# A hybrid S5/mLSTM encoder step on one core: the first FFN by Strassen's algorithm and by weight rows, the S5 weights made elsewhere

## The chip, the cores and the metric

The kernel runs on one core of a Trainium2 chip. The metric is the device time of one execution in microseconds (us). Engines: PE multiplies matrices into PSUM, eight banks of 128 x 512 fp32; DVE (VectorE), ACT (ScalarE) and POOL (GpSimd) do element-wise work; SP only issues DMAs here, and POOL and ACT issue some too. Each engine takes its instructions in the order of its own queue.

## The reference

One layer of a streaming encoder over 1072 frames (16 learned meta frames, 1024 prompt frames, 32 frames of a second stream) of width 1024, all in fp32:

```python
x = x + 0.5 * swiglu(rmsnorm(x), gate1, up1, down1)        # swiglu(x) = (silu(x@gate) * (x@up)) @ down, inner width 2816
proj = rmsnorm(x) @ w_in                                   # u, xm, z, 1024 each
y5 = s5_mix(u)      # 64 groups of 16 channels, a diagonal complex recurrence of 64 states each, then GELU and GLU
ym = mlstm_mix(xm, z)   # causal conv, block-diagonal q/k/v, gates, matrix memory of 4 heads in chunks
x = x + concat(rmsnorm(y5), rmsnorm(ym)) @ w_out
x = x + 0.5 * swiglu(rmsnorm(x), gate2, up2, down2)
return rmsnorm(x), and the final states of both streams
```

## The kernel before, in words

Everything is kept transposed: `x` is eight tiles of 128 channels x 1072 tokens. A product of two fp32 matrices is made of three matmuls in a reduced type, since each operand is split in a high part (ACT, rounding) and a low part (DVE, the rest): high x high, high x low, low x high. A weight tile of 128 x 1024 is loaded by SP and split by `wslot` (L136, two buffers each of `wr`, `wh`, `wl`); its products with a block of tokens are one `unit` (L164, 24 matmuls into one bank).

The first FFN is `ffn` (L260). It runs over 11 groups of two of the 22 inner tiles: gate and up units for three token blocks of 358, 358 and 356, then this group's share of the down product, added to `x` on DVE (L314). `Prep` makes the norm beside it: `split` (L191) multiplies by the gain and splits, `sq` sums squares (L1482), `fin` makes a column of sums (L220), a reciprocal root on DVE and a row over all partitions (L230). The last group goes block by block, so that the next norm is made beside it.

Into the first FFN a generator `fill` is woven, two or three steps per inner tile: first `ml_fold` (L680; eight times four small matmuls that fold the q, k, v matrices), then `s5_prep` (L505). That one makes tables of the recurrence on DVE and ACT (`s5_tables`, L418), and then for each of 16 batches of four groups: loads of B and C (`raw`, one buffer, eight DMAs on SP), products on POOL into `bb`, `cc`, `lb`, `wo` (L511), on PE the kernel matrix `kp` and four transposes `wps` (L556, L568), which are evicted and stored as `strip` and `win_d`, and the rotation tables `E`, seven doublings and a rest of six products each on POOL, stored as `rot_d`.

The input projection for the mLSTM (`ml_in`, L705) runs over eight 128-channel tiles: a unit for each block, the convolution on DVE (L721), small products `vp` and `gp`, stores of v by POOL's queue. Then `ml_gates` is a long chain on DVE.

The second FFN has its gate and up by `gate_up` (L336) and the class `Strassen` (L1251): pairs of inner tiles, the contraction cut in two halves, the tokens in two pairs of quarters of 264. Per pair of weight tiles and pair of quarters there are 7 products of 12 matmuls (L1376) instead of 8. `weights` makes sums of quarters of the weights on POOL and DVE (L1346 to L1349) and splits them; `late` and `early` make the operand sets of `x`. The result goes to DRAM as `h_d`. `down` (L374) then keeps all eight output tiles of a token block in the eight banks and goes over the 22 weight rows (L398).

The order on each engine's queue is set by a scheduler that follows the program's order as priority and its own estimate of when each instruction is ready; `issue_after`, `behind` and `later` add an order by hand.

## Time and profile before

| | us |
|---|---|
| median of three runs | 2453.95 (2449.87 to 2455.27) |
| the profiled execution, its own time | 2452.73 |
| its span, first to last instruction | 2451.0 |
| PE, DVE, ACT, POOL busy | 2372.5, 1436.2, 861.4, 972.5 |
| mean granted clock of PE | 0.986 of full speed |

A row of the trace gives times from the start of the span. "Busy" counts the time in which at least one instruction of the engine runs; matmuls overlap, so the mean length of one (0.33 us) is longer than the pitch at which they follow each other.

### The profile page before, as it was taken

The page shows a single profiled execution, that of the slowest core. Times are in us where ns is not written, and L with a number is a line of the kernel's source. Part 1 is how long each engine was busy: PE and PEld are TensorE (multiplying, and loading weights), DVE is VectorE, ACT ScalarE, POOL GpSimd, SP SyncE. Part 2 cuts the span into 40 slices and gives each one's busy share as a digit, 9 for nine tenths or more (in the row PEclk, how much of TensorE's full clock was granted, in tenths as well). Part 3 has the DMA queues.
Part 4 walks back from the last instruction along what each step waited for, and adds up shares of the span by engine and source line. Part 5 has one row for each costly group of instructions (what it writes and reads, how often), then busy time and mean ns, then how long its engine had stood idle before and what let it go on. Part 6 is the DMA issues. An engine that isn't in the chain of part 4 may idle for free.

```text
span 2451.0 us, 40952 instructions
## 1 busy us (share of the span) xinstructions
PE 2372.5 (97%) x15656; PEld 2307.7 (94%) x15656; DVE 1436.2 (59%) x2858; ACT 861.4 (35%) x1576; POOL 972.5 (40%) x1790
## 2 busy tenths in 40 slices
PE   8999999999999999999998989999899999999998
PEld 7999999999999988979897989999899999999998
DVE  6446444444444665635778787487765656545663
ACT  5112111111111433323544414564543434334542
POOL 3003777877877522112215262122544444420010
PEclk9999999999999999999999999999899999999999
DMA  4111222242222333252235563122222222265653
GB/s 155 56 50 57 73 75 78 78 113 75 69 78 72 103 119 60 79 161 71 70 133 177 175 191 120 52 66 89 74 75 84 74 84 75 75 209 188 228 180 110
DMA packets 163469, 254.17 MB, mean 104 GB/s; under 512 B 38289, under 2 KB 108961, under 8 KB 163273
## 3 DMA queue, kind: packets, MB, share of 16 engines
q1 hardware_dynamic: 144392, 219.85, 28.7%
q0 software_dynamic: 10032, 27.32, 3.2%
q10 hardware_dynamic: 8848, 4.38, 0.7%
q8 instruction: 123, 2.02, 0.3%
q14 instruction: 74, 0.60, 0.1%
HBM read 192.96 MB, written 62.72 MB: 104 GB/s over the span
## 4 chain that ended last, share of the span: by engine, by line
PE 68%; POOL 11%; DVE 9%; DMA 5%; issue 4%; ACT 2%; SPq 1%; POOLq 0%; ACTq 0%; DVEq 0%
PE psg L161 35%; PE psg L1376 18%; PE psd L398 7%; POOL E L511 3%; POOL et L511 2%; DMA win_d<-wi 1%; PE psg L410 1%; DVE xl L197 1%; PE cps L916 1%; DMA rb<-rb_d 1%; PE nu L884 1%; POOL wo L511 1%; PE vp L730 1%; POOL lb L511 1%; DVE xl L1287 1%
## 5 line engine op out<-in xcount | busy, mean ns | idle before, releaser
L161 PE MATMUL psg<-xh,wh 128*128 128x358 f32 (+4 forms) x2272 | 428.0, 327 | 8.7 <-ACT xh L196 7.9
L161 PE MATMUL psg<-xl,wh 128*128 128x358 f32 (+4 forms) x2272 | 421.8, 325 | 0.0
L161 PE MATMUL psg<-xh,wl 128*128 128x358 f32 (+4 forms) x2272 | 419.2, 324 | 0.0
L161 PEld LDWEIGHTS psg<-xh,wh 128*128 128x128 f32 x2272 | 371.4, 190 | 18.9 <-ACT xh L196 9.7
L161 PEld LDWEIGHTS psg<-xl,wh 128*128 128x128 f32 x2272 | 371.8, 190 | 4.9 <-issue 4.4
L161 PEld LDWEIGHTS psg<-xh,wl 128*128 128x128 f32 x2272 | 371.1, 189 | 3.7 <-issue 3.3
L153 ACT ACTIVATE wh<-wr 128x1024 fp32r<-128x1024 f32 (+1 forms) x182 | 190.9, 1049 | 401.8 <-PE psg L161 266.7
L154 DVE TENSOR_TENSOR wl<-wr,wh 128x1024 fp32r<-128x1024 f32 (+1 forms) x182 | 229.1, 1259 | 121.3 <-ACT wh L153 84.0
L314 DVE SCALAR_TENSOR_TENSOR x<-psg,x 128x358 f32<-128x358 f32 (+1 forms) x264 | 137.9, 528 | 99.3 <-PE psg L161 98.7
L161 PE MATMUL psg<-hh,wh 128*128 128x358 f32 (+1 forms) x528 | 133.7, 334 | 0.9 <-DVE x L314 0.9
L161 PE MATMUL psg<-hl,wh 128*128 128x358 f32 (+1 forms) x528 | 132.1, 329 | 0.0
L161 PE MATMUL psg<-hh,wl 128*128 128x358 f32 (+1 forms) x528 | 129.9, 327 | 0.0
L349 POOL TENSOR_TENSOR sil<-sil,Ra 128x264 f32<-128x264 f32 x88 | 79.1, 914 | 120.6 <-ACT sil L348 120.5
L398 PE MATMUL psd<-hh,wh 128*128 128x360 f32 x352 | 113.8, 327 | 0.7 <-ACT hh L370 0.7
L398 PE MATMUL psd<-hl,wh 128*128 128x360 f32 x352 | 113.8, 327 | 0.0
L273 DVE TENSOR_TENSOR gt<-psg,Ra 128x358 f32<-128x358 f32 (+1 forms) x66 | 34.9, 529 | 128.2 <-PE psg L161 120.8
L1232 POOL TENSOR_TENSOR x<-x,Rb 128x360 f32<-128x360 f32 (+1 forms) x11 | 10.9, 1018 | 245.4 <-ACT Rb L231 245.4
L282 DVE TENSOR_TENSOR hf<-sil,psg 128x358 f32<-128x358 f32 (+1 forms) x66 | 34.8, 527 | 123.4 <-PE psg L161 123.4
L1482 POOL TENSOR_TENSOR acc<-acc,sq 128x358 f32<-128x358 f32 (+2 forms) x36 | 38.5, 1069 | 170.5 <-ACT sq L1480 169.9
L511 POOL TENSOR_TENSOR et<-E 128x8 f32<-128x8 f32 (+6 forms) x256 | 92.8, 362 | 19.1
L161 PEld LDWEIGHTS psg<-hh,wh 128*128 128x128 f32 x528 | 92.5, 190 | 2.5 <-DVE x L314 2.3
L161 PEld LDWEIGHTS psg<-hl,wh 128*128 128x128 f32 x528 | 94.3, 190 | 0.0
(422 smaller groups left out, 4979.3 us busy)
## 6 DMA issues: line engine op xcount, KB each, us to landing
wr<-w2f SPq DMA_DIRECT2D x44, 512.0 KB
wr<-win SPq DMA_DIRECT2D x24, 512.0 KB
h_d<-sil SPq DMA_DIRECT2D x88, 132.0 KB
wr<-w1g SPq DMA_DIRECT2D x22, 512.0 KB
wr<-w1u SPq DMA_DIRECT2D x22, 512.0 KB
wr<-w1d SPq DMA_DIRECT2D x22, 512.0 KB
x<-w2g SPq DMA_DIRECT2D x22, 512.0 KB
x<-w2u SPq DMA_DIRECT2D x22, 512.0 KB
```

Source lines behind the costliest of these rows:

```text
L153: nc.scalar.activation(vh, r, AF.Copy)
L154: nc.vector.tensor_tensor(vl, r, vh.bitcast(F32), op=ALU.subtract)
L161: self.nc.tensor.matmul(ps[:, :n], lhsT=a[k], rhs=b[k], start=i == 0, stop=i == 3 * nk - 1)
L197: nc.vector.scalar_tensor_tensor(l, s, gain, h.bitcast(F32), op0=ALU.mult, op1=ALU.subtract)
L273: nc.vector.tensor_tensor(gt[:, :n], ps[:, :n], R[:, t0:t0 + n], op=ALU.mult)
L282: nc.vector.tensor_tensor(hf[:, :n], sil[:, :n], ps[:, :n], op=ALU.mult)
L314: nc.vector.scalar_tensor_tensor(xs, ps[:, :n], 0.5, xs, op0=ALU.mult, op1=ALU.add)
L349: nc.gpsimd.tensor_tensor(g, g, r, op=ALU.mult)
L398: nc.tensor.matmul(ps[o][:, :n], lhsT=l[:, o * P:(o + 1) * P], rhs=r, start=f == i == 0 and l is w[0], stop=f == NF - 1 and l is w[1])
L511: PT = lambda o, x, y, op: nc.gpsimd.tensor_tensor(o, x, y, op=op)
L1376: nc.tensor.matmul(ps[c, bank], lhsT=l[:, k * P:(k + 1) * P], rhs=r[k], start=start and i == k == 0, stop=i == 2 and k == 3, skip_group_ch ...
L1482: e.tensor_tensor(d, d, sq, op=ALU.add)
```

## The change

In the first FFN, gate and up go through `Strassen` with quarters of 268 tokens. `x` is loaded in quarters; `ready` adds the squares and multiplies by the gain in place, and `sets` makes all seven operand sets of both halves at the start. The result goes to a DRAM tile; `x`, overwritten by then, is loaded again in `down1`, which goes by weight rows over three blocks of 358, 358 and 356. The products on POOL of `s5_prep` are woven into `down1`, one step per weight row. Their matmuls are a generator of their own, `s5_pairs`, behind the last matmul of `down1`, with the norm's columns and rows between them. The rotation tables (`s5_rot`, eight groups at once, half of the products on DVE) and `ml_fold` go one step per tile into the input projection. `win_d` and `rot_d` are stored by SP's queue. In the second FFN the held products of the first pair come out after its third product of the second half, not after the first. The weights' host layout changes with it.

```diff
+    def row(self, ps, f, w, h, n):
+        for l, rs in zip(w, (h, h[:1])):
+            for o in range(8):
+                for i, r in enumerate(rs):
+                    self.nc.tensor.matmul(ps[o][:, :n], lhsT=l[:, o * P:(o + 1) * P], rhs=r, start=f == i == 0 and l is w[0], stop=f == NF - 1 and l is w[1])
+
+    def down1(self, x, h_d, wf, blks, post, filler):
+        todo = []
+        for j, (t0, n) in enumerate(blks):
+            ps = self.banks()
+            for f in range(NF):
+                h = self.h_load(h_d, self.hp, f, t0, n, blks[0][1], bufs=4)
+                self.row(ps, f, self.wslot(wf[f]), h, n)
+                if f > 1 and todo:
+                    i, o = todo.pop(0)
+                    post.split(i, o)
+                    post.sq(i, o)
+                if j == 0 and f in range(6, 14):
+                    self.nc.sync.dma_start(x[f - 6], self.a["xT"][f - 6])
+                next(filler, None)
+            for o in range(8):
+                xs = x[o][:, t0:t0 + n]
+                self.nc.vector.scalar_tensor_tensor(xs, ps[o][:, :n], 0.5, xs, op0=ALU.mult, op1=ALU.add)
+                todo.append((j, o))
...
+    def s5_pairs(self, pool):
+        nc, N = self.nc, 4
+        for b in range(16):
+            lb, cc = self.lb[:, b], self.cc[:, b]
...
-            wi = pool.tile([P, 512], F32, tag="lb2", name="wi")
+            wi = lb.rearrange("p g s h -> p (g s h)")
             nc.scalar.activation(wi, wps, AF.Copy)
-            nc.gpsimd.dma_start(self.win_d[b].rearrange("(h s) x -> s h x", s=8), wi)
...
+            nc.sync.dma_start(self.win_d[b].rearrange("(h s) x -> s h x", s=8), wi)
+            yield
+
+    def s5_rot(self, pool):
+        nc, N = self.nc, 8
...
+                t, u = (pool.tile([P, N, 64], F32, tag=n_, name=n_)[:, :, :m] for n_ in ("et", "eu"))
...
-                PT(t, ej(1), en(1), ALU.mult)
-                PT(eo(0), ej(0), en(0), ALU.mult)
-                PT(eo(0), eo(0), t, ALU.subtract)
-                t = pool.tile([P, N, 64], F32, tag="et", name="et")[:, :, :m]
+                VT(u, ej(1), en(1), ALU.mult)
+                VT(eo(0), ej(0), en(0), ALU.mult)
+                VT(eo(0), eo(0), u, ALU.subtract)
                 PT(t, ej(0), en(1), ALU.mult)
                 PT(eo(1), ej(1), en(0), ALU.mult)
                 PT(eo(1), eo(1), t, ALU.add)
...
+            st = Strassen(self, W1, xa, xn, Rb, hp)
+            st.open("right", 6)
...
+            def ready(c, q, k):
+                t0 = W1 * (2 * c + q)
+                xs, r = x[k][:, t0:t0 + W1], Ra[:, t0:t0 + W1]
+                if k == 0:
+                    nc.scalar.activation(r, xs, AF.Square)
+                else:
+                    sq = hp.tile([P, W1], F32, tag="sq", name="sq", bufs=2)
+                    nc.scalar.activation(sq, xs, AF.Square)
+                    (nc.gpsimd if k % 2 else nc.vector).tensor_tensor(r, r, sq, op=ALU.add)
+                nc.vector.tensor_scalar(xs, xs, self.v(V_FFN1, k), None, op0=ALU.mult)
...
+            w = st.weights((a["w1g"][0], a["w1g"][1]), lambda: (x_load(0), x_load(1, (0,))))
+            s0 = st.sets(0)
+            for i, n in enumerate((2, 1, 2, 1, 1)):
+                st.w0 = next(w)
...
+                for _ in range(n):
+                    next(s0)
...
+            self.down1(x, h_d[0], a["w1f"], blk, post, self.s5_prep(sp))
+            with self.later():
+                for b, _ in enumerate(self.s5_pairs(sp)):
+                    if b in (2, 5, 8):
+                        post.cols(b // 3)
+                    if b in (4, 7, 10):
+                        post.rows()
...
+                fold, rot = self.ml_fold(mp, mpa, pb), self.s5_rot(pb)
+                next(fold)
+                next(rot)
                 for k in range(8):
+                    next(fold, None)
                     w = self.wslot(a["win"][8 + k])
...
                     self.ml_in(k, w, xn, Rb, blk, pb, xc[k])
+                    next(rot, None)
...
         for i in range(7):
             step(i, 1)
-            if i == 0:
-                rows()
-                for h in held:
-                    out(*h)
+            if i == 2:
+                flush((0, 1) if self.ready is None else (0,))
+            if i == 3 and holds:
+                rows = rest(1)
+            if i == 6 and holds:
+                flush((1,))
```

## Rows read from the trace of the kernel before

**Rows 1.** Page of before, parts 1 and 4: busy us by engine; the chain's shares.
```profile
PE 2372.5 (97%) x15656; PEld 2307.7 (94%) x15656; DVE 1436.2 (59%) x2858; ACT 861.4 (35%) x1576; POOL 972.5 (40%) x1790
...
PE 68%; POOL 11%; DVE 9%; DMA 5%; issue 4%; ACT 2%; SPq 1%; POOLq 0%; ACTq 0%; DVEq 0%
```

**Rows 2.** Windows: stretch, its us, busy (x count) of PE PEld DVE ACT POOL, PEclk, DMA, GB/s.
```profile
6.26:55.00 48.74, 43.26 (x227) 41.33 (x228) 37.59 (x78) 29.41 (x60) 18.58 (x21) 0.89 0.50 162
...
200.00:855.30 655.30, 640.31 (x3919) 635.83 (x3918) 314.80 (x592) 136.15 (x215) 488.85 (x1257) 0.99 0.26 78
...
855.30:1005.50 150.20, 149.66 (x875) 128.00 (x873) 86.81 (x194) 47.66 (x84) 41.82 (x61) 1.00 0.36 93
...
1742.40:2176.40 434.00, 434.00 (x3577) 433.80 (x3576) 263.54 (x406) 178.26 (x365) 197.19 (x175) 1.00 0.27 87
...
2177.10:2351.00 173.90, 173.86 (x1057) 173.86 (x1058) 92.17 (x128) 82.69 (x123) 0.00 (x0) 1.00 0.62 204
```

**Rows 3.** Windows of line L161 on PE in the first FFN: stretch, us, busy (count).
```profile
619.93:631.72 11.79, 11.79 (x74) 1.00 0.15 47
```

**Rows 4.** Timeline of PE where the input projection begins: start, us, what.
```profile
855.30 1.49 PE L161 MATMUL psg<-xh,wh 128*128 128x358 f32 x8
...
867.98 0.81 PE L230 MATMUL R<-ident,ry 128*128 128x128 f32 x6
```

**Rows 5.** Timeline of DVE and POOL before and in the second FFN's first pair.
```profile
1695.71 0.43 DVE L1287 TENSOR_TENSOR B11l<-x,B11h 128x264 fp32r<-128x264 f32 x1
...
1696.22 0.76 POOL L1281 TENSOR_TENSOR x<-x 128x264 f32<-128x264 f32 x1 [9.85 <-DVE B11l L1287]
...
1717.12 8.62 DVE L1287 TENSOR_TENSOR xl<-x,xh 128x264 fp32r<-128x264 f32 x12
...
1717.63 7.14 POOL L1281 TENSOR_TENSOR x<-x 128x264 f32<-128x264 f32 x8 [6.66 <-DVE xl L1287]
...
1726.01 8.83 DVE L1287 TENSOR_TENSOR xl<-x,xh 128x264 fp32r<-128x264 f32 x11
```

**Rows 6.** Groups of DVE in the second FFN's down: busy us, mean ns, idle before.
```profile
L154 DVE TENSOR_TENSOR wl<-wr,wh 128x1024 fp32r<-128x1024 f32 x43 | 52.7, 1225 | 67.9 <-ACT wh L153 41.4 <-PE psd L398 26.5
...
L371 DVE TENSOR_TENSOR hl<-hr,hh 128x360 fp32r<-128x360 f32 x44 | 23.2, 528 | 1.2 <-ACT hh L370 1.1
```

**Rows 7.** Windows of POOL from 200 to 850: all, then tile E alone.
```profile
200.00:850.00 650.00, 485.54 (x1253) 0.99 0.26 79
...
200.00:850.00 650.00, 275.54 (x862) 0.99 0.26 79
```

**Rows 8.** Timeline of the S5 tables: first DVE product, a first POOL product of prep.
```profile
198.85 0.23 DVE L420 TENSOR_TENSOR mag<-lamr,ldt 128x64 f32<-128x64 f32 x1 [0.56 <-ACT ldt L427]
...
208.75 0.29 POOL L511 TENSOR_TENSOR pt<-raw,lami 128x64 f32<-128x64 f32 x1 [0.36 <-DVE lami L479]
```

**Rows 9.** Waits of SP's queue, 200 to 850: us in total, times, longest.
```profile
SPq L526 <- POOL cc L542: 105.1, 14, 10.5
...
SPq L539 <- POOL bb L511: 18.0, 2, 13.6
```

**Rows 10.** Waits of PE, 40 to 856: us in total, times, longest.
```profile
PE kp L556 <- POOL lb L511: 14.0, 9, 3.6
```

**Rows 11.** Timeline of PE, one batch of S5 matmuls and what follows.
```profile
269.75 0.96 PE L556 MATMUL kp<-cc,lb 128*128 128x16 f32 x8
...
270.95 1.54 PE L161 MATMUL psg<-xh,wh 128*128 128x358 f32 x8
```

**Rows 12.** Timeline of PE, one step of the fold and what follows.
```profile
73.94 0.31 PE L697 MATMUL fp<-gq,bd 128*128 128x36 f32 x2
...
74.75 0.58 PE L161 MATMUL psg<-hh,wh 128*128 128x358 f32 x2
```

**Rows 13.** Group of DVE, 855 to 1006: busy us, mean ns, idle before.
```profile
L721 DVE SCALAR_TENSOR_TENSOR cv<-xm,vec,cv 128x1075 f32<-128x1075 f32 x24 | 31.8, 1330 | 1.5 <-ACT cv L719 1.5
```

**Rows 14.** Group of ACT, 855 to 1006.
```profile
L734 ACT ACTIVATE vs<-vp 128x256 f32<-128x256 f32 x8 | 3.1, 385 | 31.0 <-DMA v_d<-vs 24.3 <-PE vp L730 3.9 <-PE psg L161 2.8
```

More of the change, by code (lines that the diff above doesn't have):

```diff
@@ L49, in cuts @@
         t += 2 * q
-    return out
-def down_slots(groups):
-    out, f, off = [], 0, 0
-    for gi, g in enumerate(groups):
-        no = 2 if g == 3 else 4
-        for o in range(0, 8, no):
-            out.append((gi, f, g, o, no, off))
-            off += P * no * g * P
-        f += g
     return out
@@ L372, in h_load, with banks, down @@
         return hh, hl
-    def down(self, x, wf, wd, pool, post):
+    def banks(self):
+        return [(self.psg if o % 2 == 0 else self.psm)("psd") for o in range(8)]
+    def row(self, ps, f, w, h, n):
[21 more added lines that the diff above has]
+                todo.append((j, o))
+        for _ in filler:
+            pass
+        for i, o in todo:
+            post.split(i, o)
+        for i, o in todo:
+            post.sq(i, o)
+    def down(self, x, h_d, wf, wd, pool, post):
         nc, blks = self.nc, post.blks
@@ L1303, in early, with late, sets @@
             self.split(0, "T4", k, b21)
-    def late(self, c):
-        if c == 0:
-            for k in (2, 3):
-                self.split(0, "T4", k, self.rows(0, k)[2])
-            return
-        r = [self.rows(1, k) for k in range(4)]
+    def late(self):
+        for k in (2, 3):
+            self.split(0, "T4", k, self.rows(0, k)[2])
+    def sets(self, c):
+        r = [self.rows(c, k) for k in range(4)]
         for n in self.OPS:
             for k, (b11, b12, b21, b22) in enumerate(r):
+                if self.ready is not None and n in ("B11", "B21", "T1", "T2"):
+                    self.ready(c, n[0] == "T", k + 4 * (n in ("B21", "T2")))
                 if n == "T1":
@@ L1366, in gemm @@
                 K.behind(es, 20)
-                self.late(1)
+                for _ in self.sets(1):
+                    pass
         ps, u, held = {}, {}, []
+        holds = set() if rest is None else {0, 1}
         def mm(c, bank, a, b, start=True):
@@ L1383, in emit @@
         def emit(n, c, q, t):
-            if rest is not None and c == 0:
+            if c in holds:
                 held.append((n, c, q, t))
@@ L1416, in gemm, with flush @@
             step(i, 0)
-        rows = rest()
+        rows = rest(0)
+        def flush(cs):
+            rows()
+            holds.difference_update(cs)
+            for h in held:
+                if h[1] in cs:
+                    out(*h)
         for i in range(7):
             step(i, 1)
-            if i == 0:
-                rows()
-                for h in held:
-                    out(*h)
+            if i == 2:
[4 more added lines that the diff above has]
+                flush((1,))
 class _Spare:
```

298 lines of the change are left out of this document (133 added, 165 removed).

## The prediction

> **What bounds the kernel now.** First the busy times and the chain that ended last: PE is busy 97% of the span and holds 68% of the chain [rows 1]. The reader is to see that a saving must be made in PE's time, or in the gaps of its queue. Second the same by stage [rows 2]: the first FFN (6.26 to 855.3) is PE-bound after its start, the start is not (43.3 of 48.7 us busy at a granted clock of 0.89, and a busy PE there is often a slow one), and the second FFN's gate and up, which already go by Strassen, keep PE busy in all 434.0 us of their steady part. Third PE's pitch, stage over matmuls (an edge of such a window counts one or two matmuls too many): first FFN 11.79/72 = 0.1638 us for three units of 358, 358 and 356 columns; Strassen at 264 columns 434.0/3577 = 0.1213; down by weight rows at 360 columns 173.9/1057 = 0.1645 [rows 2, 3].
>
> **The change, part by part.** All against the profiled execution: span 2451.0, its own time 2452.7, which is 1.2 under the median 2453.95 of three runs. I follow PE's clock to the point where the input projection is alone on PE. Before that is 855.3 plus the three blocks' norm columns and rows still to come, 0.81 for a block's rows [rows 4] and about as much for its columns, together some 4: 859.2.
>
> *Start.* Before, PE's first matmul comes at 6.26, behind one tile of weights and one block of x [rows 2]. After, the first pair of weight tiles needs all seven operand sets of both token halves, made while PE waits. DVE is the longest: per half 28 splits, 16 gain multiplications, 6 additions of squares. One split alone takes 0.43, and POOL's subtraction alone 0.76; side by side, 23 splits take 17.45, 0.76 each [rows 5]. So 28 x 0.76 = 21.2; the additions are like a split, 6 x 0.43 = 2.6; a gain multiplication has no row: under a split's 0.43, over half of it, I take 0.35, 5.6. Two halves 58.8, the weights' own two wide (1.22 [rows 6]) and five half-wide operations (between 0.43 at 264 and 1.22 at 1024 columns: 0.69) 5.9, start at about 6. End of the first pair: 70. Ends: 50 if nothing slows the splits, 86 if POOL's 48 operations of 0.76 all stand in DVE's way.
>
> *Gate and up.* 3168 matmuls at 0.1638 become 22 weight pairs x 2 halves x 7 products x 12 = 3696. At 268 columns the pitch lies between 0.1213 and, by columns, 0.1213 x 268/264 = 0.1231, which I take. The 21 pairs after the first: 3528 x 0.1231 = 434.3, to 504. DVE, ACT and POOL have the same work beside it as in the second FFN, 61%, 41% and 45% busy there [rows 2]; that cover holds.
>
> *Down.* 1584 matmuls stay 1584; by rows at 0.1645 they take 260.6 (before 259.5). With 1 us of hand-over (the two stages of the second FFN lie 0.7 apart [rows 2]): 766.
>
> *S5 weights beside down.* Before, POOL is busy 485.5 between 200 and 850, 275.5 of it with the rotation tables (tile E) [rows 7]. What stays beside down is the rest of 210, less the issue of win_d, which moves to SP: I take 200, in 261 instead of 650 us. In front stand the lambda tables, DVE and ACT work before POOL's first product, 198.85 to 208.75 before [rows 8], 13 with the loads. DVE's operations on two SBUF tiles in that stage: 66 x (1.225 + 0.528) = 116 [rows 6], and 14 for 24 splits and squares like the second. 12 splits and 8 subtractions would take 11.2 one after the other and took 8.62, 0.77 of that [rows 5]; (200 + 130) x 0.77 + 13 = 267 against 261. So POOL has no slack here, where before it was 75% busy. It reaches PE by SP's queue: the loads of `raw`, one buffer, wait for POOL, and behind them stand the loads of weight and h rows. Before, SP stood at these loads 237 us in 30 waits, 7.9 each [rows 9] (the first and the last of four such rows), harmless with one weight load per 12 us. Now a weight row is eaten every 24 x 0.1645 = 3.95 us; two slots are a reserve of 7.9. I take 8 us for the stage, since the mean wait is just the reserve. Ends: 0, and 32 waits as long as the longest at L526, 10.5: 32 x 2.6 = 83. x is loaded a second time (4.4 MB) in eight of these steps; the second FFN does so at the same place, moved 204 GB/s in its stage with PE unbroken [rows 2], so it costs nothing. If that cover goes, one load of 0.5 MB stands before each weight row, 1 to 2 us each.
>
> *Pairs.* The K and win matmuls leave the first FFN with the waits of kp for lb, 14.0 [rows 10]; their PE time stays, 1.2 per group of four (269.75 to 270.95) [rows 11], 16 x 1.2 = 19.2, now behind the last down matmul. With the norm columns and rows between them 4, and 6 for eight evictions of 0.53 (as hl [rows 6]) that free the banks, with splits and squares on DVE: 29. Ends 23 and 45; the input projection's first four units can fill in, further ones wait for a row of Rb. At 8 + 29 behind 766: 803 against 859.2, that is 56 gained.
>
> *Input projection.* The folded q, k, v matmuls come here: 0.81 on PE per k (73.94 to 74.75) [rows 12], 8 x 0.81 = 6.5. The rotation tables come too, half on DVE, 8 batches of 8 doublings x 3 operations on each engine. POOL's 275.5 us are 862 operations of four groups each; after there are eight groups in each and half of the products go to DVE, so a quarter of the operations and half of the elements stay: between 69 and 138, I take the middle, 104. DVE: 0.69 at 512 columns, 0.43 at 264, the rest of the eight widths less each, about 2.3 for the eight; x 3 x 8 = 55. In this stage DVE was 86.8 and POOL 41.8 of 150.2 [rows 2]; that makes 142 and 146. It fits, with nothing over. By 0.77: (31.8 [rows 13], 8 x 1.22 [rows 6] and 55 of DVE on two tiles, 104 of POOL) = 201 x 0.77 = 154, 4 late. Behind a rotation step on POOL queue the v_d stores; for those ACT already waits 24.3 with its copies out of PSUM [rows 14]. On DVE the evictions that free PE's banks and the gates' chain queue behind it. I take 14. Ends 0 and 201 - 150 = 51.
>
> The second FFN's edit (the rows of its norm two products later) is put at nothing: other products stand in the gap.
>
> Sum: -56 + 6.5 + 14 = -35.5, 2452.7 - 35.5 = 2417.
>
> **A rule against it.** DVE's split goes from 0.43 to 0.72 and 0.80 beside POOL [rows 5], so the two hinder each other, but 20 operations still overlapped to 0.77 of their sum. The Trainium skill, "SBUF — State Buffer", section "Who interferes with whom", is harsher: a DVE instruction with two SBUF inputs and a GpSimd instruction that reads SBUF share a port under an exclusive lock, and the second one blocks fully. The trace agrees that they block, not that nothing overlaps. Taken strictly it is the rival "turns" below.
>
> **Rivals.** *Everything fits* (chance 0.20): no stall in down, none by the rotations, banks free in time: 2417 - 8 - 14 - 6 = 2389; with the short start 2369. For it: POOL and DVE work that took no PE time before; against it: both stages come out at 94 to 102% full.
>
> *Turns* (0.05): DVE and POOL never overlap. Down's helpers take 200 + 130 + 13 = 343, 82 late instead of 8; rotations 51 instead of 14; start 86 instead of 70: 2417 + 74 + 37 + 16 = 2544. Against it: 8.62 for 11.2 [rows 5], and 263.5 + 197.2 busy in 434.0 us without a gap on PE [rows 2].
>
> *SP's queue* (0.12), slower than before: in the down stage the raw loads hold up weight rows. Price up to 83 instead of 8: 2417 + 75 = 2492. It decides from (36 + 8)/32 = 1.4 us beyond the reserve per wait. For it: 7.9 mean, 10.5 longest at L526, up to 13.6 at L539 [rows 9]; against: a wait is long where SP had nothing else to do, as it had before.
>
> *It doesn't do what it says* (0.03): narrow matmuls cost as much as wide ones. Then 3528 x 0.041 is lost, 2560; 0.1213 speaks against it [rows 2].
>
> **How the numbers follow.** Forecast 2417 (0.60), its own range 2398 to 2440 from the start's and the pairs' ends. A measurement of this kernel tells about 0.2% (5 us) from no change. Faster: 0.58 of the forecast, 0.20, and 0.02 of SP's queue in a mild form, 0.80. Same: 0.02 + 0.04 + 0.01 = 0.07. Slower: 0.06 + 0.05 + 0.02 = 0.13. The range 2380 to 2462 reaches into everything fits and into half of SP's queue.
>
> **What would show it.** Right: steady gate and up at 0.123 per matmul; the first pair done near 70; down at 0.165 with few gaps; first input projection matmuls near 770 and alone near 800; no kp wait over a few us. Wrong: PE waiting for wl or hh in down with SP at raw; kp waiting for lb; PE below 95% in the input projection with DVE near 100%; a later stage that loses what the first gains.

## The result, and the profile after

The changed kernel takes 2521.3 us (median of 4 runs, 2518.6 to 2524.0) against 2454.6 for the kernel before on the same chip: ratio 1.0274, 95% interval 1.0252 to 1.0296. It is slower by 67 us, where 2417 was forecast and the range ended at 2462. One execution each of experiments 1, 4 and 14 was far longer than its fellows (8924.8, 5033.4 and 2640.1) and is left out of the medians below. The profiled execution has a span of 2521.6, 70.6 longer than [rows 1].

The page of after, busy times and chain, against [rows 1]: PE is busy 5.5 us less, and idle 155 us instead of 79, which is the growth of the span. POOL's largest rows in the chain are `lt` and `wo`, S5 products.

```profile
PE 2367.0 (94%) x16196; PEld 2288.9 (91%) x16196; DVE 1604.6 (64%) x3104; ACT 1015.3 (40%) x1926; POOL 1061.2 (42%) x1336
...
PE 60%; DVE 14%; POOL 11%; issue 6%; DMA 5%; ACT 2%; SPq 1%; POOLq 0%; DVEq 0%; ACTq 0%
PE psg L1414 34%; PE psg L148 10%; PE psd L287 9%; POOL lt L449 2%; PE psg L348 2%; POOL wo L449 2%; POOL lbs L449 1%; DVE xl L1307 1%; PE cps L872 1%; POOL E L534 1%; PE nu L840 1%; POOL bb L449 1%; DMA rb<-rb_d 1%; DVE wl L141 1%; DMA rot_d<-E 1%
```

The forecast followed PE from stage to stage, so the loss is found by the same marks, read from the timelines of PE: first down matmul, last down matmul, last transpose of the gates (`gtp`, end of the input projection), last `nu` (end of the mLSTM). The last two of before are 1008.9 and 1240.1; its down and norm were taken to end at 859.2.

| stretch on PE | forecast | after | difference |
|---|---|---|---|
| start, gate and up, to the first down matmul | 504 | 523.3 | +19 |
| down | 270 | 308.8 (to 832.1) | +39 |
| pairs, entry, input projection, to the last `gtp` | 199 (29 + 149.7 + 6.5 + 14) | 226.8 (to 1058.9) | +28 |
| gates and chunks, to the last `nu` | 231.2, as before | 250.7 (to 1309.6) | +19.5 |
| the rest | as before | 1.1 longer | +1 |

Together 106, which is the forecast's -35.5 turned into +70.6. Windows of after: stretch, its us, busy (count) of PE, PEld, DVE, ACT, POOL, PE's granted clock, DMA share, GB/s.

```profile
0.00:70.00 70.00, 38.40 (x163) 31.40 (x164) 63.83 (x111) 35.88 (x90) 45.74 (x54) 0.92 0.38 124
70.00:95.00 25.00, 20.66 (x111) 19.59 (x112) 17.86 (x37) 11.40 (x28) 10.52 (x11) 0.68 0.07 19
95.00:520.00 425.00, 425.00 (x3445) 425.00 (x3445) 248.67 (x392) 172.07 (x351) 186.43 (x165) 1.00 0.25 78
523.30:832.30 309.00, 275.48 (x1588) 271.03 (x1587) 182.76 (x274) 115.34 (x173) 236.80 (x375) 0.96 0.56 183
580.00:620.00 40.00, 33.63 (x193) 32.75 (x192) 20.04 (x18) 12.62 (x18) 37.91 (x62) 0.96 0.57 185
700.00:740.00 40.00, 35.67 (x196) 35.10 (x197) 26.88 (x31) 18.39 (x31) 38.06 (x62) 0.91 0.56 184
870.00:900.00 30.00, 20.00 (x91) 19.59 (x91) 4.97 (x22) 4.59 (x7) 4.54 (x19) 0.52 0.58 128
```

The reader is to see four things: a start with PE half idle; a steady stretch as forecast (425.0/3445 = 0.1234 us per matmul, 0.1231 forecast); a down stage (523.3 to 832.3) in which PE is idle for 33.5 us and has a mean clock of 0.96, so that its busy time grows too, while POOL is full at 95% in the two windows of 40 us; and 30 us before the input projection with PE idle for a third, at a granted clock of 0.52.

Groups of DVE in the start of after, shapes apart, with mean ns of one:

```profile
L1307 DVE TENSOR_TENSOR xl<-x,xh 128x268 fp32r<-128x268 f32 x32 | 20.6, 667 | 0.0
L952 DVE TENSOR_SCALAR x<-x,vec 128x268 f32<-128x268 f32 x32 | 19.1, 619 | 0.0
L951 DVE TENSOR_TENSOR Ra<-Ra,sq 128x268 f32<-128x268 f32 x12 | 6.8, 563 | 0.0
```

SP's waits from 580 to 835 (us in total, times, longest), and ACT's group for the high parts of the weights in the whole of down:

```profile
SPq L139 <- DVE wl L141: 40.0, 21, 3.5
SPq L466 <- POOL cc L482: 34.1, 14, 5.3
SPq L479 <- POOL bb L449: 24.7, 8, 6.2
SPq L479 <- POOL pt L449: 13.5, 6, 3.7
```
```profile
L140 ACT ACTIVATE wh<-wr 128x1024 fp32r<-128x1024 f32 x67 | 70.9, 1059 | 172.0 <-DMA wr<-w1f 120.3 <-PE psd L287 38.2 <-DVE hl L276 5.3
```

SP stands 72 us at the loads of `raw` for POOL, the weight rows come late behind them (120 us of ACT's idle time ends with a landing weight row), and PE waits for ACT. These are the waits of [rows 9], smaller in sum and each (2.6 in the mean of 28, 6.2 the longest), but now in front of PE. SP's timeline, with the wait of PE that follows:

```profile
588.36 0.38 SPq L139 DMA_DIRECT2D wr<-w1f  x1
...
592.38 2.39 SPq L479 DMA_DIRECT2D raw<-s5c  x4
594.87 0.53 SPq L139 DMA_DIRECT2D wr<-w1f  x1
...
599.77 3.18 SPq L466 DMA_DIRECT2D raw<-s5b  x4
603.00 0.58 SPq L139 DMA_DIRECT2D wr<-w1f  x1
...
608.11 0.43 PE L287 MATMUL psd<-hh,wh 128*128 128x358 f32 x1 [3.90 <-ACT wh L140]
```

From 588.36 to 603.00 one weight row goes out between the two at the ends, where PE eats one in 3.95: two waits for POOL and the issue of eight loads (5.6) stand there. In the whole of down the issue of the 128 loads holds SP for 76 us (0.59 each in the median), as long as its waits for POOL do (77).

The timeline where the input projection begins:

```profile
880.58 1.73 PE L514 MATMUL kp<-ccs,lbs 128*128 128x16 f32 x8
...
882.59 4.74 SPq L523 DMA_DIRECT2D strip<-ks  x8
...
887.44 0.58 SPq L529 DMA_DIRECT2D win_d<-lbs  x1
888.07 1.89 SPq L1017 DMA_DIRECT2D tg_d<-strip  x3
...
892.08 0.11 POOL L539 MEMSET E<- 128x8 f32 x1 [83.44 <-DMA tg_d<-strip]
...
892.14 0.59 DVE L1007 MEMSET GM<- 128x640 f32 x1 [9.58 <-DMA tg_d<-strip]
...
892.66 0.52 DVE L669 TENSOR_TENSOR xm<-psg,Rb 128x358 f32<-128x358 f32 x1
...
893.24 2.16 PE L148 MATMUL psg<-xh,wh 128*128 128x358 f32 x6 [10.01 <-DVE xm L669]
```

`E`, `GM` and `xm` lie where the S5 weights (`lbs`, one tile for all batches) were, so they wait for the last store out of it. DVE stands at GM's memset, and behind it on the queue are the evictions `xm` that free PE's banks. POOL, which was to make rotation tables, has been idle for 83 us.

Behind the input projection some two batches of tables are left, and stand in the queues of DVE, POOL and SP ahead of the gates. Windows of tile E alone in the gates of after (DVE and POOL busy):

```profile
1058.90:1139.70 80.80, 24.21 (x58) 42.27 (x69) 0.96 0.40 133
```

From the last `gtp` to the first `ktp` are 80.8 us instead of 42.0. PE does units of the S5 input there, work that it has to do later in any case, so that only half of it is lost.

### The profile page after: what moved, and what is told of

Read it like the earlier page. It is cut to its first block, busy times and chain, and to the rows that moved or that the text cites. A ratio compares the mean times of both kernels' runs of the same rounds, so it can differ in the third digit from the quotient of the medians.

```text
span 2521.6 us, 43211 instructions
## 1 busy us (share of the span) xinstructions
PE 2367.0 (94%) x16196; PEld 2288.9 (91%) x16196; DVE 1604.6 (64%) x3104; ACT 1015.3 (40%) x1926; POOL 1061.2 (42%) x1336
## 4 chain that ended last, share of the span: by engine, by line
PE 60%; DVE 14%; POOL 11%; issue 6%; DMA 5%; ACT 2%; SPq 1%; POOLq 0%; DVEq 0%; ACTq 0%
PE psg L1414 34%; PE psg L148 10%; PE psd L287 9%; POOL lt L449 2%; PE psg L348 2%; POOL wo L449 2%; POOL lbs L449 1%; DVE xl L1307 1%; PE cps L872 1%; POOL E L534 1%; PE nu L840 1%; POOL bb L449 1%; DMA rb<-rb_d 1%; DVE wl L141 1%; DMA rot_d<-E 1%
## 5 line engine op out<-in xcount | busy, mean ns | idle before, releaser
L287 PE MATMUL psd<-hh,wh 128*128 128x358 f32 (+2 forms) x880 | 291.6, 335 | 30.5 <-ACT wh L140 24.8
L287 PE MATMUL psd<-hl,wh 128*128 128x358 f32 (+2 forms) x880 | 290.2, 333 | 0.0
L148 PE MATMUL psg<-xh,wh 128*128 128x352 f32 (+4 forms) x1216 | 226.7, 324 | 11.8 <-DVE xm L669 10.0
L148 PE MATMUL psg<-xl,wh 128*128 128x352 f32 (+4 forms) x1216 | 228.9, 325 | 0.0
L148 PE MATMUL psg<-xh,wl 128*128 128x352 f32 (+4 forms) x1216 | 221.8, 322 | 0.0
L148 PEld LDWEIGHTS psg<-xh,wh 128*128 128x128 f32 x1216 | 195.2, 192 | 16.7 <-DVE xm L669 10.4
L148 PEld LDWEIGHTS psg<-xl,wh 128*128 128x128 f32 x1216 | 197.6, 193 | 7.6 <-issue 7.3
L287 PEld LDWEIGHTS psd<-hh,wh 128*128 128x128 f32 x880 | 170.2, 194 | 34.6 <-ACT wh L140 28.4
L148 PEld LDWEIGHTS psg<-xh,wl 128*128 128x128 f32 x1216 | 195.7, 191 | 1.1 <-issue 0.8
L287 PEld LDWEIGHTS psd<-hl,wh 128*128 128x128 f32 x880 | 170.4, 194 | 0.0
```

What stands on the lines that cost most here:

```text
L148: self.nc.tensor.matmul(ps[:, :n], lhsT=a[k], rhs=b[k], start=i == 0, stop=i == 3 * nk - 1)
L287: self.nc.tensor.matmul(ps[o][:, :n], lhsT=l[:, o * P:(o + 1) * P], rhs=r, start=f == i == 0 and l is w[0], stop=f == NF - 1 and l is w[1])
```

## The experiments

Ratios are to the kernel before on the same chip, with the 95% interval; after stands at 1.0274.

**1. Is it SP's queue?** Loads of B and C only for the first of 16 batches; the others compute with those values.

```diff
-            raw = new("raw", 2)
+            if b == 0:
+                raw = new("raw", 2)
...
-            craw = new("raw", 2)
+            if b == 0:
+                craw = new("craw", 2)
```

> Left out: the loads of B and C for 15 of the 16 batches; every batch computes with the first one's. POOL's products, DVE's work and the weight rows stay as they are; only the loads that made SP's queue wait for POOL are gone. Changed kernel: down from 523.3 to 832.8, 309.5 us where 1584 matmuls at 0.1645 are 260.6; PE idle in it about 31, granted clock 0.91 to 0.96 in between. If SP's queue is the cause (weight rows behind loads that wait for POOL): idle of PE in the down stage below 5, down 262 to 268, the time 41 to 49 shorter, 2472 to 2481. If DVE and POOL hinder each other at SBUF so that the splits of the weights come late: PE still waits for wh and wl, down stays above 295, the time within 10 of 2521.

1.0109 (1.0081 to 1.0137), 2484.4. Down takes 275.9 instead of 308.8. POOL is as full as before:

```profile
580.00:620.00 40.00, 40.00 (x246) 40.00 (x245) 22.60 (x25) 16.62 (x23) 38.34 (x54) 1.00 0.60 204
...
740.00:780.00 40.00, 40.00 (x247) 40.00 (x246) 22.37 (x22) 16.86 (x22) 38.19 (x55) 1.00 0.63 209
```

So 33 of the 47 us that down takes over the 262 of experiment 16 are SP's queue. The other 14 (262 to 268 was expected here) stay while POOL makes its products; PE waits 6.5 once for `wh` and 5.0 in two waits for `wl`, and what makes them was not tested. "Turns" falls as well: DVE's work in down takes 145.8 with POOL almost idle (experiment 16) and POOL's some 200 by the forecast, which one after the other would not fit in 275.9.

**2. The rotation tables** left out (memsets in place of the six products).

```diff
-                VT(u, ej(1), en(1), ALU.mult)
...
-                PT(eo(1), eo(1), t, ALU.add)
+                nc.gpsimd.memset(eo(0), 0.5)
+                nc.gpsimd.memset(eo(1), 0.5)
```

> Left out: the products of the rotation tables (constants are stored in their place, by the same queue, from the same tile). From the end of down to the last gate transposes the changed kernel took 29 us more than forecast, and the gates behind them cost 17 more. If the rotations' work on DVE and POOL and the waits for it are the cause: 35 to 50 us shorter, 2471 to 2486. If most of it is the wait of DVE at the entry of the stage (PE idle 10 us for xm, then a granted clock of 0.52) the gain is only 10 to 22: 2499 to 2511, and the 10 us wait stands in the trace as before.

1.0168 (1.0150 to 1.0186), 2498.0: between the two expectations, nearer to the second. The last `gtp` comes only 3 us earlier, while the gates are back at 42.1, and DVE's wait at the entry stands as before (PE waits 10.0 for `xm`). The tables cost about 23 us, nearly all in the gates, not in the input projection. Without the products their stores come in a burst, so the 23 is not a clean price.

**3. The gain multiplication** of the start on ACT.

```diff
-                nc.vector.tensor_scalar(xs, xs, self.v(V_FFN1, k), None, op0=ALU.mult)
+                nc.scalar.activation(xs, xs, AF.Copy, scale=self.v(V_FFN1, k))
```

> The 32 multiplications by the norm's gain at the start go from DVE (0.62 each, 19 us of the 82 in which it is busy without a gap) to ACT. If DVE's queue sets the start: the first pair's last matmul 10 to 16 us earlier than 93.5, the time 8 to 16 shorter, 2505 to 2513. If ACT, with the high parts and the squares, becomes as late (43 of 94 us busy, 13 more), or the transfers of x set it: within 4 of 2521.

1.0217 (1.0201 to 1.0232), 2509.6. The first pair ends at 88.6 instead of 93.5, down begins at 518.4 instead of 523.3. The time lies in the first branch, and in part by luck: the start gives 4.9 where 10 to 16 were expected, and 9 come from the gates and chunks (241.9 for 250.7).

**4. The same products spread** over twice as many weight rows.

```diff
-                next(filler, None)
+                if f % 2 == 0 or j == 0 and f < 2:
+                    next(filler, None)
```

> One step of the S5 weights per two weight rows in place of one per row, over the whole down stage (33 steps for 66 rows); nothing left out. If SP's queue is the cause, the loads of B and C now come at POOL's own pace (about 14.5 us a batch against 4 x 3.95 = 15.8), the down stage loses below 10 us, and the time is 38 to 49 shorter, 2472 to 2483. If the pairs' matmuls then wait for POOL's last batches, up to 20 of it are given back: 2483 to 2503, with waits of kp for lb. If the cause is contention at SBUF: within 10 of 2521.

A miss: 1.0245 (1.0224 to 1.0265), 2516.4; SP still stands 69.5 at POOL's `cc`, `pt` and `bb` between 580 and 835 and down takes 303.8. The edit did not change the order on SP: the batches' first loads go out at 532, 564, 584, 599, 613, and at 532, 565, 585, 600, 614 in after. The place in the program is only a priority; that the scheduler's estimate of POOL is too fast is my reading of it, not shown.

**5. Loads tied to their weight row** on SP, one batch ahead, at the pace of 4, in five buffers (`pin` sets the order behind SP's last DMA).

```diff
+        def load(b):
+            with self.pin():
+                for n in ("s5b", "s5c"):
+                    out.append(pool.tile([P, 2, N, H5], F32, tag="raw" + n, name="raw", bufs=5))
...
+            raw, craw = nxt
+            nxt = load(b + 1) if b < 15 else None
```

> Nothing left out. The loads of B and C get five buffers each instead of one, come one batch ahead, one batch per four weight rows, and are tied on SP's queue behind the weight row before them, so that the scheduler can't draw them forward to where it thinks that POOL will be free. If SP's queue is the cause of the long down stage, this gives what leaving the loads out gave: down 262 to 276 instead of 308.9, the time 32 to 45 shorter, 2476 to 2489, and SP's waits for POOL below 10 us in all. If POOL's work as such is the limit (239 busy of 309), its last batches come after the last weight row and the pairs wait for lb: down 262 to 276, but kp waits of 10 to 25 behind it, 2490 to 2505.

Down misses both branches: 1.0186 (1.0164 to 1.0208), 2501.3; down 288.0. Three batches of eight DMAs, some 0.6 us each, stand in a row on SP at the beginning and hold a weight row up, for which PE waits 12.8:

```profile
550.00:580.00 30.00, 21.26 (x114) 21.26 (x115) 21.25 (x70) 8.96 (x13) 16.29 (x31) 0.77 0.59 180
```

**6. As 5, one DMA per batch** (B and C laid out together on the host).

```diff
+                nc.sync.dma_start(t, a["s5bc"][:, b])
```

> As the one with pinned loads, but B and C of a batch come in one DMA instead of eight (the host lays them out so); nothing else. With eight DMAs a batch, SP needed 5 us to issue them, three batches in a row stood before the third weight row (PE idle 12.8 there), and down took 288 against 276 without the loads. If that is SP's issue time: down 268 to 278, the time 30 to 40 shorter than the changed kernel, 2481 to 2491. If it is the transfers themselves that hold up the weights (many small pieces): down still above 284, 2497 to 2504.

1.0138 (1.0119 to 1.0158), 2489.8; down 272.0. With 16 loads on SP instead of 128 (9 us of issue instead of 76), down is 16 us shorter than in 5, and 10 us over the 262 of experiment 16. The new layout makes the pieces of a load larger too (1 KB of a partition in place of 256 bytes), so issue and transfer are not told apart.

**7. Memory.** The S5 weights in 16 tiles, two buffers for `ks`, the tables `E` on the other side, where the rows of h had been.

```diff
-        self.lb = pool.tile([P, 16, N, 8, H5], F32, name="lbs")
+        self.lb = [pool.tile([P, N, 8, H5], F32, name=f"lbs{b}") for b in range(16)]
...
-                fold, rot = self.ml_fold(mp, mpa, pb), self.s5_rot(pb)
+                fold, rot = self.ml_fold(mp, mpa, pb), self.s5_rot(rp)
```

> Nothing left out. The S5 weights lie in 16 tiles instead of one, ks gets two buffers, and the rotation tile E and its two scratch tiles lie where the h rows of the down stage were, instead of on the S5 weights: so the first eviction of xm need not wait for the last store of win_d, and POOL can begin the rotations at about 832 instead of 892, where it now stands idle for 83 us. If the wait at the entry and the lateness of the rotations (two batches in the gates' way, 80.8 from the last gate transpose to the first chunk's ktp against 42.0 before) are the cause: the wait of 10 for xm goes, the gates take 42 to 48, the time 28 to 45 shorter, 2476 to 2493. If the rotations, drawn into the pairs, stand on DVE in the way of ks and xm (each doubling waits for the other engine): less than 15 gained, 2506 or more.

1.0156 (1.0133 to 1.0178), 2494.0. The tables begin in the stage of the pairs and are done in time: the gates are back at 41.7, with the last `gtp` 4 later (1063.3). The wait for `xm` stays at 8.6, now because a batch of rotations stands ahead of it on DVE's queue.

**8. 3, 5 and 7 together**, and the second load of x tied to its rows too.

```diff
-                    self.nc.sync.dma_start(x[f - 6], self.a["xT"][f - 6])
+                    with self.pin():
+                        self.nc.sync.dma_start(x[f - 6], self.a["xT"][f - 6])
```

> Both edits and the gain on ACT together, and the second loads of x tied on SP's queue behind weight rows 6 to 13 instead of all at the start of the stage. If the losses are separate, they add up: 12 + 38 + 35 and 3 to 6 for the loads of x, 2428 to 2442, faster than before. If they share what they hide (an earlier end of down leaves POOL's prep to end behind it, and the rotations with it): 2445 to 2460.

Above both expectations: 1.0090 (1.0065 to 1.0114), 2478.0; `gtp` 1042.5, gates 41.8. PE waits 10.7 for `xm`, again behind rotations on DVE.

**9. As 8, all rotations on POOL.**

```diff
-        VT = lambda o, x, y, op: nc.vector.tensor_tensor(o, x, y, op=op)
+        VT = PT
```

> As the one with everything, but all products of the rotations on POOL, none on DVE: about 170 us of POOL between the end of down and the gates (220 us with v's stores, 42). If DVE's queue in the input projection is what the rotations cost: 3 to 12 faster than with both engines. If POOL then becomes the limit (its products took 0.55 to 0.65 us in the mean beside DVE, which makes 230): rotations end in the gates again, 5 to 20 slower than with both.

1.0156 (1.0127 to 1.0185), 2492.3. `gtp` comes 18 us earlier (1024.6), the gates take 88.7: POOL's tables run to 1100, and the stores that the gates wait for stand behind them. No rotation stands on DVE's queue, and still PE waits 14.8 for `xm`: DVE's small memset of `xm` waits for a DMA, as in after. The last pairs run at full clock here (0.96 for eight `kp`, 1.73 in after).

```profile
844.71 0.96 PE L528 MATMUL kp<-ccs,lbs 128*128 128x16 f32 x8
...
860.39 0.06 DVE L678 MEMSET xm<- 128x3 f32 x1 [13.74 <-DMA tg_d<-strip]
```

**10. As 9, with one DMA per batch as in 6**, the S5 weights laid out last batch first, two buffers for `E`, the weights of the fold in a free tile of x, the gates' stores by ACT.

```diff
-            E = pool.tile([P, 2, N, SCOL], F32, tag="E", name="E", bufs=1)
+            E = pool.tile([P, 2, N, SCOL], F32, tag="E", name="E", bufs=2)
...
-        nc.gpsimd.dma_start(self.rb_d[0:NH], b)
+        nc.scalar.dma_start(self.rb_d[0:NH], b)
```

> Everything that the runs so far pointed to: one DMA a batch, the gain on ACT, x's second loads tied to weight rows, the S5 weights in 16 tiles laid out last batch first (so that the first xm lies on batches stored long before), all rotations on POOL with two buffers of E (with one, POOL waited 6 to 8 us for each store), the gates' rows stored by ACT's queue instead of POOL's. If the losses are what the runs say: down 268 to 276, no wait for xm, the last gate transpose at 995 to 1012, gates of 42 to 50, and 2425 to 2452, faster than before or level. If the rotations on POOL again end in the gates and hold up the first chunk: 2455 to 2475.

Above both expectations: 1.0184 (1.0170 to 1.0198), 2500.5. The wait for `xm` is gone (0.55; PE waits 4.3 for `bd`). The input projection ends at 999.8, 9 us before that of the kernel before, and all of it is given back: PE waits for `bq`, whose work stands behind the tables on POOL.

```profile
836.60 2.75 PE L155 MATMUL psg<-xh,wh 128*128 128x358 f32 x8 [0.55 <-DVE xm L678]
```
```profile
PE ktp L810 <- DMA bq<-bqk: 35.8, 1, 35.8
```

**11 to 15. The share of DVE and POOL.** Whole batches, instead of half of each, go to one engine: three of eight to DVE in the first.

```diff
-        PT = lambda o, x, y, op: nc.gpsimd.tensor_tensor(o, x, y, op=op)
+            e = nc.vector if b in (1, 3, 5) else nc.gpsimd
+            PT = VT = lambda o, x, y, op, e=e: e.tensor_tensor(o, x, y, op=op)
```

> As the best guess before it (there the input projection ended at 999.8, 9 before the kernel before, and then the first mLSTM chunk waited 35.8 for rotations still on POOL until 1100), but rotation batches 1, 3 and 5 wholly on DVE and the other five wholly on POOL, so that neither waits for the other inside a batch; and every second bd tile in a free row of x. Five batches on POOL at about 27 plus v's stores 27 make some 165 us from 812, so they end near 1000, before the gates. If that is the whole trouble: last gate transpose 995 to 1012, gates 42 to 48, first chunk at 1038 to 1058, the time 2438 to 2454, faster than before or level. If DVE's three batches (about 19 each) stand in the way of xm's evictions: last gate transpose 1012 to 1030, 2454 to 2470.

1.0029 (1.0019 to 1.0039), 2462.6, the second branch; the gates take 52.8. PE waits 9.9 for a load of the fold (`bd`). Then four of eight on DVE, and the fold's loads by ACT:

> As the version with the rotations split between the engines (2462.6), where PE still waited 9.9 for the fold's bd, whose load stood on SP's queue behind 16 stores of strip and the loads of tg_d, 5.8 for wh, and rotations on POOL still ended in the gates (gates 52.8): bd and bdv are loaded by ACT's queue, the copies into tg_d come after each tile's ml_in in the program, and every second rotation batch (four) is on DVE. If SP's issue time at the entry is the rest of the loss: no wait for bd, last gate transpose at 998 to 1008, gates 42 to 47, the time 2440 to 2452, faster than before. If the pairs' half clock and DVE's rotations keep it: last gate transpose 1010 to 1018, 2453 to 2462.

1.0009 (0.9999 to 1.0019), 2461.0, again the second branch; the wait for `bd` stays at 9.8, so that it is not for SP; I read it as a wait for the place of a late-stored S5 weight, and 14, which gives `bd` another place, bears that out. Beside it, the start's twelve additions of squares from DVE to POOL:

> As the one before it, and the 12 additions of squares that DVE does at the start (0.56 each) go to POOL too. If DVE's queue is still what sets the start, with the gain already on ACT: gate and up end 3 to 6 earlier, the time 3 to 6 shorter. If the three engines are now level (DVE 58, ACT 53, POOL 49 of the first 70) and POOL's subtractions, on which the T sets wait, come later: 0 to 6 longer.

1.0027 (1.0017 to 1.0037), 2464.1; down begins 2.3 later than in the one before: that fits POOL being as full as DVE in the start. Then three of eight on DVE, `bd` in free tiles of x, and POOL's tables stored by POOL's own queue:

```diff
-            bd = ... else wpool.tile([P, 3, P], F32, tag="bd", name="bd", bufs=1)
+            bd = (x7[:, 640:1024] if k % 2 else x6[:, 264:648]).rearrange("p (i j) -> p i j", i=3)
```

> As the version level with the kernel before (2461.0, ratio 1.0009), where PE still waited 9.8 for bd (its tile lay on an S5 weight that was stored late): both bd tiles lie in free rows of x, bd and bdv are loaded by SP again; three rotation batches on DVE (1, 3, 5) and five on POOL, and POOL stores its own by its own queue, since E's second buffer was held until SP, busy with some 40 stores of 0.6 each, had sent the first. If SP's issue at the entry is the rest of the loss: no wait for bd, rotations done before 1010, last gate transpose 995 to 1006, gates 42 to 48, the time 2440 to 2451, faster than before. If the half clock of the pairs and DVE's work hold it: last gate transpose from 1010, 2452 to 2460.

0.9984 (0.9971 to 0.9997), 2452.6: the best version, 69 us under the change and within 0.2% of the kernel before. No wait for `bd`; 12.4 for `xm`, the last `gtp` at 1010.0 and gates of 60.0. And that with four of eight on DVE:

> As the one before it with four batches on each engine. If POOL's five end in the gates there: gates 5 to 10 shorter here and the time 3 to 8 shorter. If DVE's fourth batch stands in the gates' own chain, which is DVE's: 3 to 10 longer.

1.0000 (0.9989 to 1.0012), 2455.5, with gates of 60.7: level with the one before it, as far as the intervals tell.

**16. How much was there to be had?** The change with all S5 products, their loads and the rotations left out (memsets in their place), stores, matmuls and the rest as they are.

```diff
-            PT(bb[:, 0], raw[:, 0], bc(cr), ALU.mult)
...
+            nc.gpsimd.memset(self.cc[:, b], 0.01)
+            nc.gpsimd.memset(self.lb[:, b], 0.01)
```

> Left out of the changed kernel: all products and loads of the S5 weights (constants are written and stored in their place) and the products of the rotations; the pairs' matmuls, stores, tables and everything else stay. It shows what the change is worth when the moved S5 work costs nothing. If SP's queue and the rotations are the whole loss behind the start: down 262 to 268, gates 42, and by the sum of what each alone gave (38 to 45 and 24) 2452 to 2460, still no faster than before, since the start and the entry of the input projection (10 for xm at half clock) stay. If the pairs and the entry suffer from the S5 work as well: 2425 to 2448.

0.9990 (0.9978 to 1.0001), 2453.1. Down takes 262, as priced, the gates 40.8. But the start is 16 us longer than forecast, and from down's end to the last `gtp` are 223.5 us, 38 more than the 185 forecast without rotations. Even with the S5 products free the change gains nothing. Windows of down, the entry up to the wait for `xm`, and the input projection; PE in the gap; and the wait in it, DVE's as in after:

```profile
520.10:782.00 261.90, 259.64 (x1587) 259.33 (x1586) 145.83 (x274) 118.53 (x173) 29.77 (x71) 1.00 0.62 207
782.00:842.17 60.17, 48.80 (x326) 47.89 (x324) 22.03 (x85) 18.80 (x36) 1.17 (x15) 0.76 0.66 185
842.17:1005.50 163.33, 154.86 (x874) 129.56 (x874) 77.09 (x177) 43.08 (x73) 57.68 (x211) 0.96 0.59 147
...
820.00:860.00 40.00, 29.96 (x159) 29.20 (x159) 12.97 (x29) 10.05 (x14) 9.31 (x48) 0.66 0.72 147
```
```profile
841.07 0.59 DVE L964 MEMSET GM<- 128x640 f32 x1 [9.61 <-DMA tg_d<-strip]
```

**17 and 18. What does `xm` wait for?** The version with `bd` in x, with the stores taken off SP: `strip` by ACT, `win_d` by POOL; then also the copies to `tg_d` behind the gates in the program.

```diff
-                    nc.sync.dma_start(st[:, :, (14 - i) * H5:(15 - i) * H5], kall[i * H5:(i + 1) * H5])
+                    nc.scalar.dma_start(st[:, :, (14 - i) * H5:(15 - i) * H5], kall[i * H5:(i + 1) * H5])
...
-            nc.sync.dma_start(self.win_d[b].rearrange("(h s) x -> s h x", s=8), wi)
+            nc.gpsimd.dma_start(self.win_d[b].rearrange("(h s) x -> s h x", s=8), wi)
```

> f7_bd_in_x with the stores of the pairs taken off SP's queue: strip (16 DMAs) by ACT's queue, win_d (16 DMAs) by POOL's. In f7_bd_in_x PE waits 12.4 for xm; on SP there stand from 836.31 on eight strip stores (5.88), a win_d store and three tg_d copies (1.87) before the load of VG at 846.85, and DVE's copy into VG, which xm is queued behind, begins at 847.25. Theory: the issue of these DMAs on SP is what xm waits for. Then the wait falls from 12.4 to under 4 and the time by 7 to 10, to 2444 to 2448 (ratio 0.995). Rival: what is waited for is the landing of the stores (memory that comes free late); then the wait stays at 9 or more and the time within 3 of 2453.

> f9_stores_off_sp with the 64 copies from strip to tg_d (about 0.6 each on SP, 38 in all between 820 and 900) put behind the gates in the program's order. If SP's issue time holds up the input projection's loads beyond the first wait, the last gtp comes a few us earlier than in f9_stores_off_sp and the time falls by 2 to 6 more (2440 to 2446). Rival: the loads have slack once the first wait is gone, and the copies, now between the gates and the first S5 tables, hold up loads of the chunks or of S5: the same time or up to 8 longer.

Both missed on the far side: 1.0070 (1.0056 to 1.0084), 2472.4, and 1.0073 (1.0060 to 1.0086), 2473.2. PE waits 23.0 and 24.4, now in the row of the load of `xm`'s first columns. In the timeline of the first, 28 copies to `tg_d` move up on SP, the last eight `strip` stores go out on ACT only from 846.3, and the last eviction of a pair stands behind them on ACT; its store is the last `win_d`:

```profile
828.20 21.76 SPq L1028 DMA_DIRECT2D tg_d<-strip  x28
...
846.30 7.04 ACTq L533 DMA_DIRECT2D strip<-ks  x8
853.44 0.60 ACT L538 ACTIVATE lbs<-wps 128x512 f32<-128x512 f32 x1 [18.93 <-DMA strip<-ks]
...
854.33 0.60 POOL L539 DMA_DIRECT2D win_d<-lbs  x1 [18.93 <-DMA tg_d<-strip]
...
859.61 0.20 DVE L666 COPY Gc<-fp 128x36 f32<-128x36 f32 x1 [23.29 <-DMA tg_d<-strip]
```

The distance from the issue of the last `win_d` store to the DVE operation that stands ahead of `xm` is 5.3 here and 5.1 in the second. It was 4.7 in after (887.44 to 892.14) and in seven other runs (1 to 6 and 16, there from 836.37 to 841.07), and 5.0 in the versions with `bd` in x (14, 842.29 to 847.25, and 15). The last store moved by 50 us between these runs and the wait moved with it. In 17 and 18, where the trace has the landing of that store (4.4 and 4.3 after its issue), the operation begins 0.9 behind it. So it is the rival: DVE waits for the memory of the last S5 weight, free some 5 us after its store goes out; a queue matters as far as it delays that store (the eight `strip` stores stand ahead of it). Where `E` and `GM` no longer waited for it (7, 8), rotations on DVE's queue took the place of the wait. With neither, in 10, where the first tiles of the next stage lie on batches stored long before and no rotation is on DVE, PE does not wait for `xm`.

## Why the prediction was wrong

*Right.* The pitch of Strassen (0.1234 for 0.1231), down's length where nothing disturbs it (262 in experiment 16 for 261), the second FFN's edit (behind the first FFN and the mLSTM the distance between the two kernels stays at 69.5 to 70.6), the pairs' waits for `lb` (none; 1.3 for `ks`), and that DVE and POOL overlap.

*Start, 19 of 106.* "A gain multiplication has no row: under a split's 0.43, over half of it, I take 0.35." Alone it takes that (343 ns at least, 352 the median), but the mean of the 32 is 619, the longest 1374: 17 that hardly met a POOL operation took 0.34 to 0.35, the other 15, beside one, 0.84 to 1.37. The Trainium skill, "SBUF — State Buffer", section "Who interferes with whom", names `tensor_scalar` among the operations that can take the port pair shared with GpSimd; the trace agrees. The page ties that to a mode of the operation, which no run here shows. I had used the rule for DVE operations on two tiles alone. 32 x 0.27 is 9; by a count of DVE's busy time the rest of the 23 us to the first pair's end (93.5 for 70) is the second pair's weights, the norm and the silu on the same queue, which I did not count: DVE has no gap from 6 to 82. The count is not a test: experiment 3 takes all 19 us of the multiplications off DVE, and the pair ends 4.9 earlier.

*Down, 39.* "I take 8 us for the stage, since the mean wait is just the reserve." The path was right and stood as a rival, SP's queue; this term was the failing step, mis-sized at 8 where 47 (39 + 8) was lost, above the middle of my own ends, 0 and 83. Three things were wrong in it. The size of the waits was taken over from before, where 114 of the 237 us of [rows 9] were waits for the rotation tables, which the change takes out of this stage:

```profile
SPq L539 <- POOL E L586: 75.2, 10, 11.7
SPq L539 <- POOL E L585: 38.4, 4, 14.4
```

In after no wait between 580 and 835 is as long as the reserve of 7.9 (6.2 at most). It was their sum that counted: I compared one wait with the reserve, and they follow each other with only a weight row or two between them, as SP's timeline above shows. The issue of the 128 loads, 76 us of SP, was put at nothing, without a reason. And a late row was priced as idle time alone: PE is idle 33.5 us in down, and its busy time is 275.5 at a mean clock of 0.96, for 259.6 at 1.00 in experiment 16. POOL's work came to 237 instead of 200 (`wo` 874 ns for 784 before), and its first product at 556.65, 33 after down's beginning, not 13, behind the lambda tables; what these two cost was not tested alone.

*Pairs and entry, 28.* Two terms were wrong, and both show in experiment 16, without rotations, where this stretch is 38 over the forecast. The first is the entry, 60.2 (782.0 to 842.2). Some 16 of it are the projection's own first units, so it is about 16 over the forecast of 29. PE is idle 11.4, 10.0 of it the wait for memory, which I had at nothing (the 6 that I allowed were for evictions): the step that I moved brought its stores behind it, and the next stage's tiles lay on what they read. The rest is the clock. I priced the pairs at that of a full PE, and PE is busy some 17 us here at half of it: the last groups take 1.73 to 1.86 for eight `kp` instead of 0.96 [rows 11]. In after it is the same, with a granted clock of 0.52 between 870 and 900. The first ten groups, most with units of the projection between them, take 0.96 to 1.04. The clock falls where the last groups stand alone; but in experiment 9 they stood alone from 836.4 to 846 at 0.96 to 0.99, so they need not lose it, and what makes the difference was not tested. The second is the input projection, some 23 over: PE idles 8.5 in it (0.5 before [rows 2]), 8.3 of that in waits for `VG` and `GM`, which DVE writes; the mean clock is 0.96; and 40 matmuls of the next stage stand in it, about 7 us that come off later.

*Rotations, 19.5 net.* "I take 14", in the input projection, since both engines just fitted. They began 60 us after down's end (29 was forecast), for the memory, and ran into the gates, a chain that has no cover. Experiment 7 brings the gates back to 41.7 by memory alone, for 6 us more in the input projection; 9 and 10 show that on POOL alone they end in the gates again (88.7 and 119.4).

*The sum.* Each of the four was costed against the stage it was moved to, as a share of busy time. None was followed along one queue to the instruction behind it. Experiment 16 says that the error was not only in S5: with its products left out, the nearest to "everything fits", 2389, the kernel measured 2453.

## What to carry to other kernels

Where loads and waits share an in-order queue, count what holds the queue between two urgent loads, waits and issue together, not one wait against the reserve. When work is moved out from under a full PE, price it at the clock and with the memory of the place that it goes to: its stores hold tiles that the next stage needs. And a free share of an engine over a stage is not room: ask what stands behind each moved step on that queue at the moment.

## What the runs showed of the hardware

A DVE multiplication of a tile by a column (128x268) took 0.34 to 0.35 alone and 0.84 to 1.37 beside a POOL operation, 0.62 in the mean of 32. SP's time to issue a DMA did not follow the size: 0.38 for a weight row of 512 KB, 0.59 for a load of 16 KB of B or C, 0.60 for a copy of 64 KB to `tg_d`, 0.58 for a store of 256 KB (medians in after). Memory under a 256 KB store is free 4.7 to 5.3 us after the issue. Between down and the input projection the granted clock fell to 0.52 (870 to 900 of after) and 0.66 (820 to 860 of experiment 16), and the last eight-`kp` groups took 1.73 there for 0.96; with the same matmuls in experiment 9 all 16 groups took 0.96 to 1.04.
